# Seven products of halves in place of eight for the second feed-forward product, and the residual stream parked in DRAM

## Chip, cores, metric

One core of one Trainium2 chip. The metric is the device time of the whole kernel in microseconds, median of the runs shown; lower is better. Engines are named as in the profile: PE is TensorE (PEld its weight loads), DVE is VectorE, ACT is ScalarE, POOL is GpSimd, SP is SyncE, which here only issues DMAs.

## What is computed

Two layers of a transformer trunk over 512 latent tokens and 256 context tokens of 1024 channels. Each layer has four mixers on one input projection, an output projection with a residual layer norm, and then a feed-forward block with a second residual layer norm. The change touches only the feed-forward block:

```python
def channel_mlp(h, w1, w2):
    return jnp.square(jax.nn.relu(h @ w1)) @ w2
...
x = layer_norm_affine(DN_ALPHA * x + m[2] * y, ln1_g[l], ln1_b[l])
f = channel_mlp(modulate(x, m[3], m[4]), w_ff1[l], w_ff2[l])
x = layer_norm_affine(DN_ALPHA * x + m[5] * f, ln2_g[l], ln2_b[l])
```

`w_ff1` is 1024 x 4096, `w_ff2` is 4096 x 1024, all float32. In layer 0 the context tokens go through the same block, so N = 768 rows; in layer 1 only the latent tokens do, N = 512.

## The kernel before

**Arithmetic.** A float32 product is made of three products in the type fp32r: each operand is split into a high part (an ACT copy into fp32r) and a low part (a DVE subtraction, operand minus high part), and `mm3` (L135) issues high x high, high x low, low x high into the same PSUM bank. A "split" below is this pair of one ACT and one DVE instruction; for a weight piece it is `load_w` (L154), ACT at L162, DVE at L165, on 128 x 1024 elements.

**Order.** The program is written as straight code; a planner takes the instructions in about program order, whichever is ready first by its own timing model, and fixes each engine's queue. On the chip every queue runs in that fixed order, with waits on semaphores.

**Feed-forward block, `ffn` (L181).** The 4096 hidden columns go in eight chunks `c` of 512. `ff1(c)` (L208) makes four hidden tiles of 128 columns x N tokens: 24 matmuls of 512 columns each, in layer 0 another 24 of 256 columns, into a two-bank PSUM tile from `P2`; ACT evicts it with a relu into `r` (`T` tile); `square` (L201) makes the high part on ACT and, with two DVE instructions, the low part, in two `Z` tiles. `ff2(c, fs)` (L1277) multiplies by 512 rows of `w_ff2`: for each half `n` of the 1024 output columns and each token tile (6 in layer 0, 4 in layer 1) `ff2_tile` (L1262) issues 4 x 3 matmuls of 512 columns into one bank from `PA`, then DVE multiplies the bank by the gate row (L1274) and adds it to the residual tile `x` or `xc` in SBUF (L1275). The loop at L1299 issues `ff1(c + 1)` ahead of `ff2(c)`. In chunk 7 `ff2` goes tile by tile, POOL does the additions, and `done(j)` (L1448) starts the closing layer norm of the tile.

**Pools of tiles.** `pw` (`N_W` = 8) holds four weight pieces as high and low parts, `pr` (`N_RAW` = 4) four raw pieces as loaded, `pz` (`N_Z` = 18) the 128 x 768 `Z` tiles, `pt` (`N_T` = 6) the `T` tiles, `px` 6 tiles for `x` and `xc`, `pg` 4 `G` tiles of 128 x 1024 for gate and norm rows. PSUM has 3 banks in `PA`, 1 in `PF`, 2 x 2 in `P2`. A tile that reuses a slot waits until the last reader of the former one is through. Weights come by DMA on SP's queue (`load`, L114), gate and norm rows on ACT's queue (`bcast_rows`, L1304), where `rows2` (L1437) fetches all four.

## Time and profile before

| | us |
|---|---|
| median of 3 runs | 1571.38 (1569.65 to 1572.05) |
| profiled execution, its time | 1570.16 |
| its span | 1568.4 |
| PE busy | 1481.3 (94% of the span) |
| DVE busy | 922.7 (59%) |
| ACT busy | 565.7 (36%) |
| POOL busy | 222.0 (14%) |

Busy time is the union of an engine's instructions over the span. The feed-forward matmuls run from about 382 to 924 us (layer 0) and from about 1202 to 1553 us (layer 1); the mixers, with POOL's softmax scaling among them, lie outside these stretches.

### The profile page before, as it was taken

The page shows a single profiled execution, that of the slowest core. Times are in us where ns is not written, and L with a number is a line of the kernel's source. Part 1 is how long each engine was busy: PE and PEld are TensorE (multiplying, and loading weights), DVE is VectorE, ACT ScalarE, POOL GpSimd, SP SyncE. Part 2 cuts the span into 40 slices and gives each one's busy share as a digit, 9 for nine tenths or more (in the row PEclk, how much of TensorE's full clock was granted, in tenths as well). Part 3 has the DMA queues.
Part 4 walks back from the last instruction along what each step waited for, and adds up shares of the span by engine and source line. Part 5 has one row for each costly group of instructions (what it writes and reads, how often), then busy time and mean ns, then how long its engine had stood idle before and what let it go on. Part 6 is the DMA issues. An engine that isn't in the chain of part 4 may idle for free.

```text
span 1568.4 us, 23456 instructions
## 1 busy us (share of the span) xinstructions
PE 1481.3 (94%) x9438; PEld 1246.7 (79%) x9438; DVE 922.7 (59%) x1615; ACT 565.7 (36%) x1000; POOL 222.0 (14%) x244
## 2 busy tenths in 40 slices
PE   5899889999999999999999989989998999999996
PEld 3689677787988888888888868867776888888885
DVE  4385755547545445454454798675645656655557
ACT  4433555524621221312113156355625433222322
POOL 1021334223000000000000062143222000000003
PEclk9999999999999999999999999999998999999998
DMA  8441366362232121211211223235363433333221
GB/s 296 152 120 55 112 219 195 108 242 89 81 108 65 49 76 54 76 59 55 81 55 67 81 94 111 64 109 178 120 208 108 147 95 95 95 101 92 88 81 54
DMA packets 148069, 169.93 MB, mean 108 GB/s; under 512 B 8776, under 2 KB 96248, under 8 KB 147960
## 3 DMA queue, kind: packets, MB, share of 16 engines
q1 hardware_dynamic: 137912, 149.94, 30.7%
q10 hardware_dynamic: 10048, 18.49, 3.5%
q8 instruction: 74, 1.21, 0.3%
q14 instruction: 35, 0.29, 0.1%
HBM read 164.19 MB, written 4.22 MB: 107 GB/s over the span
## 4 chain that ended last, share of the span: by engine, by line
PE 84%; DVE 7%; DMA 3%; ACT 2%; issue 1%; POOL 1%; SPq 0%; ACTq 0%; POOLq 0%; DVEq 0%
PE ff L133 54%; PE wo L133 5%; PE wb L133 3%; PE o L133 3%; PE pT L188 2%; PE wa L133 2%; PE ada L133 2%; PE wp L133 2%; PE wu L133 2%; PE wq L133 2%; PE sm L133 2%; DMA wada<-in_w_ada 1%; DVE nmax L533 1%; PE wk L133 1%; PE hT L188 1%
## 5 line engine op out<-in xcount | busy, mean ns | idle before, releaser
L162 ACT ACTIVATE hiw<-raww 128x1024 fp32r<-128x1024 f32 x120 | 126.8, 1062 | 565.8 <-PE ff L133 565.8
L165 DVE TENSOR_TENSOR low<-raww,hiw 128x1024 fp32r<-128x1024 f32 x120 | 146.3, 1223 | 245.3 <-ACT hiw L162 245.3
L133 PE MATMUL ff<-low,fh 128*128 128x512 f32 x640 | 249.0, 389 | 0.0
L133 PE MATMUL ff<-hiw,fl 128*128 128x512 f32 x640 | 249.0, 389 | 0.0
L133 PE MATMUL ff<-hiw,fh 128*128 128x512 f32 x640 | 247.9, 389 | 0.0
L133 PE MATMUL ff<-hl,hiw 128*128 128x512 f32 (+1 forms) x672 | 237.9, 354 | 0.0
L133 PE MATMUL ff<-hh,hiw 128*128 128x512 f32 (+1 forms) x672 | 237.8, 354 | 0.0
L133 PE MATMUL ff<-hh,low 128*128 128x512 f32 (+1 forms) x672 | 237.7, 354 | 0.0
L1274 DVE TENSOR_TENSOR fft<-ff,gate 128x512 f32<-128x512 f32 x160 | 110.0, 687 | 100.2 <-PE ff L133 100.2
L133 PEld LDWEIGHTS ff<-hh,hiw 128*128 128x128 f32 x672 | 127.1, 189 | 17.9
L133 PEld LDWEIGHTS ff<-hl,hiw 128*128 128x128 f32 x672 | 127.1, 189 | 17.7
L133 PEld LDWEIGHTS ff<-hh,low 128*128 128x128 f32 x672 | 127.0, 189 | 17.7
L133 PEld LDWEIGHTS ff<-hiw,fl 128*128 128x128 f32 x640 | 120.1, 188 | 25.0
L133 PEld LDWEIGHTS ff<-hiw,fh 128*128 128x128 f32 x640 | 120.2, 188 | 24.8
L133 PEld LDWEIGHTS ff<-low,fh 128*128 128x128 f32 x640 | 120.1, 188 | 24.7
L1275 POOL TENSOR_TENSOR x<-x,fft 128x512 f32<-128x512 f32 x14 | 20.3, 1452 | 837.5 <-DVE fft L1274 832.5
L547 POOL TENSOR_SCALAR p<-p,rec 128x768 f32<-128x768 f32 (+3 forms) x80 | 63.1, 793 | 142.0 <-DVE rec L546 132.1
L1275 DVE TENSOR_TENSOR x<-x,fft 128x512 f32<-128x512 f32 x114 | 78.7, 690 | 2.9
L133 PE MATMUL ada<-wada,sc 128*32 128x128 f32 x1536 | 60.7, 295 | 20.0 <-DMA wada<-in_w_ada 20.0
L133 PEld LDWEIGHTS ada<-wada,sc 128*32 128x32 f32 x1536 | 41.8, 116 | 34.1 <-DMA wada<-in_w_ada 13.1
L188 PE MATMUL pT<-ident,p 128*128 128x128 f32 x368 | 55.9, 279 | 9.9 <-ACT pT L555 4.4
L133 PE MATMUL wo<-lowo,yh 128*128 128x512 f32 x160 | 62.5, 390 | 0.5 <-DVE lowo L165 0.5
(335 smaller groups left out, 2749.7 us busy)
## 6 DMA issues: line engine op xcount, KB each, us to landing
raww<-in_w_ff SPq DMA_DIRECT2D x120, 512.0 KB, 4.2
wada<-in_w_ada SPq DMA_DIRECT2D x96, 512.0 KB, 4.6
rawwo<-in_w_out SPq DMA_DIRECT2D x16, 512.0 KB, 6.1
rawz<-in_w_ff SPq DMA_DIRECT2D x8, 512.0 KB, 5.6
rawwb<-in_w_in SPq DMA_DIRECT2D x12, 256.0 KB, 4.1
gate<-grow ACTq DMA_DIRECT2D x6, 512.0 KB, 6.8
badab<-in_b_ada SPq DMA_DIRECT2D x36, 64.0 KB, 3.9
x<-in_x SPq DMA_DIRECT2D x4, 512.0 KB, 4.4
```

Source lines behind the costliest of these rows:

```text
L133: return self.pinned(self.nc.tensor.matmul(out, lhsT, rhs, start=start, stop=stop))
L162: i = nc.scalar.activation(out=hi, in_=raw, func=AF.Copy)
L165: nc.vector.tensor_tensor(out=lo, in0=raw, in1=hi.bitcast(F32), op=ALU.subtract)
L188: return self.pinned(self.nc.tensor.transpose(out, in_, self.ident if ident is None else ident))
L533: nc.vector.tensor_reduce(out=nm, in_=S[:, lo:hi], axis=AX.X, op=ALU.max, negate=True)
L547: nc.gpsimd.tensor_scalar(out=p[:, :keep], in0=p[:, :keep], scalar1=rec, scalar2=1.0, op0=ALU.mult, op1=ALU.mult)
L1274: nc.vector.tensor_tensor(out=t, in0=ps, in1=g[:, sl], op=ALU.mult)
L1275: eng.tensor_tensor(out=xt[:, sl], in0=xt[:, sl], in1=t, op=ALU.add)
```

## The change

For chunks 0 to 6 the product of the chunk's hidden activations (N x 512) with its 512 x 1024 weights is made by Strassen's scheme in Winograd's form. The activations are cut into halves of tokens (`half` = 384 in layer 0, 256 in layer 1; `HT` = 3 or 2 token tiles) and of hidden columns (even and odd tiles), the weights into the same halves of rows and halves of output columns. Seven products of halves, each `HT` x 2 x 3 matmuls of 512 columns, take the place of eight.

The parts: `operands` squares `r` on POOL, forms sums and differences of halves on POOL in `T` tiles, and splits seven pairs of halves on ACT and DVE, two pairs ahead of the loop body and one after each product (`more`). `weights` loads four raw quarters, forms four differences on POOL, in place, and splits seven pieces (before: four). `ff2_chunk` adds each product's banks, straight from PSUM, to one or two accumulators in SBUF: ten additions for each token tile of a half. Four quarters of the result lie in `acc` (the six `X` slots), a part common to three of them in `base` (two or one `G` tiles). In chunk 0 the first write of each is an ACT copy. Since `acc` takes the slots of the residual stream, `x` is written to DRAM (`xr`) and fetched again after the product of chunk 6; there DVE adds `base`, POOL multiplies by the gate row, DVE adds the residual. Chunk 7 stays as it was, and its `square` too, but `ff1(7)` is now issued after the product of chunk 6. The rows of the closing norm are fetched late (`rows2(1)`), since `base` takes their slots.

```diff
...
+        N = NL + NC if full else NL
+        half = N // 2
+        HT = half // 128
+
...
+                rs.append(r)
+            return rs
 
         def ff1_first():
 
...
+        def operands(rs):
+
+            pool = nc.gpsimd
+            for r in rs:
+                pool.tensor_tensor(out=r[:, :N], in0=r[:, :N], in1=r[:, :N], op=ALU.mult)
+            q = []
+            for p in range(2):
+                tmp = self.T("fsum", 768)
+                e, o = rs[2 * p], rs[2 * p + 1]
+                q.append((e[:, :half], o[:, :half], e[:, half:N], o[:, half:N], tmp[:, :half], tmp[:, half:N]))
+
+            def halves(k):
+                res = []
+                for v in q:
+                    z = self.Z("fop")
+                    hi, lo = z[:, :half], z[:, half:N]
+                    nc.scalar.activation(out=hi, in_=v[k], func=AF.Copy)
+                    nc.vector.tensor_tensor(out=lo, in0=v[k], in1=hi.bitcast(F32), op=ALU.subtract)
+                    res.append((hi, lo))
+                return res
+
+            def sums(o, a, b, op):
+                for v in q:
+                    pool.tensor_tensor(out=v[o], in0=v[a], in1=v[b], op=op)
+
+            yield halves(0)
+            sums(4, 2, 3, ALU.add)
+            yield halves(4)
+            sums(5, 4, 0, ALU.subtract)
+            yield halves(5)
+            sums(4, 1, 5, ALU.subtract)
+            yield halves(4)
+            sums(2, 0, 2, ALU.subtract)
+            yield halves(2)
+            yield halves(1)
+            yield halves(3)
+
+        def weights(c):
+
+            pool = nc.gpsimd
+
+            def raw(odd, n):
+                t = self.pr.tile([128, 2, 512], F32, name=self.nm("raww2"), tag="raw")
+                self.load(out=t, in_=w2[:, 4 * c + odd:4 * c + 4:2, 512 * n:512 * n + 512])
+                return t
+
...
+            def diff(o, a, b):
+                pool.tensor_tensor(out=o, in0=a, in1=b, op=ALU.subtract)
+
+            b11, b12, b22, b21 = raw(0, 0), raw(0, 1), raw(1, 1), raw(1, 0)
+            yield halves(b11)
+            diff(b11, b12, b11)
+            yield halves(b11)
+            diff(b11, b22, b11)
+            yield halves(b11)
+            diff(b12, b22, b12)
+            yield halves(b22)
+            yield halves(b12)
+            yield halves(b21)
+            diff(b21, b21, b11)
+            yield halves(b21)
+
+        def ff2_chunk(c, left, acc, base, more):
+
+            B = weights(c)
+            seen = set()
+
+            def add(ps, key, sl):
+                if c == 0 and key not in seen:
+                    seen.add(key)
+                    nc.scalar.activation(out=sl, in_=ps, func=AF.Copy)
+                else:
+                    nc.vector.tensor_tensor(out=sl, in0=ps, in1=sl, op=ALU.add)
+
+            for i, to in enumerate((("11", "B"), ("12", "22"), ("B",), ("12",), ("21", "22"), ("11",), ("21",))):
+                if i % 2 == 0:
+                    banks = [self.PA("ff2") for _ in range(HT)]
+                else:
+                    big = self.P2("ff2")
+                    banks = [big[:, 0:512], big[:, 512:1024]]
+                    if HT > 2:
+                        banks.append(self.PF("ff2") if i == 3 else self.P2("ff2")[:, 0:512])
+                W, a = next(B), left[i]
+                for t in range(HT):
+                    for p in range(2):
+                        self.mm3(
+                            banks[t], [h[:, 128 * t:128 * t + 128] for h in a[p]],
+                            [h[:, p, :] for h in W], p == 0, p == 1,
+                        )
+                    for q in to:
+                        if q == "B":
+                            sl = base[t]
+                        else:
+                            n = int(q[1]) - 1
+                            sl = acc[HT * (int(q[0]) - 1) + t][:, 512 * n:512 * n + 512]
+                        add(banks[t], (q, t), sl)
+                more()
 
...
-        def ff2(c, fs):
-            if c < NCH - 1:
-                for n in range(2):
-                    Ws = ff2_w(c, n)
-                    for tl in tiles:
-                        ff2_tile(fs, Ws, n, tl, nc.vector)
-            else:
-                Ws = [ff2_w(c, n) for n in range(2)]
-                self.ends = []
-                if l == 0:
-                    self.wb_first = self.wb_z(1)
-                for j, tl in enumerate(tiles):
-                    for n in range(2):
-                        eng = nc.vector if l == DEPTH - 1 and j == len(tiles) - 1 else nc.gpsimd
-                        ff2_tile(fs, Ws[n], n, tl, eng, self.last_mm if j + n else None)
-                    done(j)
-
-        cur = ff1_first()
-        gl, gc = rows2()
-        tiles = [(128 * i, x[i], gl) for i in range(LT)]
-        if full:
-            tiles += [(NL + 128 * i, xc[i], gc) for i in range(CT)]
-        for c in range(NCH):
-            nxt = ff1(c + 1) if c + 1 < NCH else None
-            ff2(c, cur)
-            cur = nxt
+        rs = ff1_first()
+        big = [self.G([128, 1024], "base") for _ in range((HT + 1) // 2)]
+        base = [big[t // 2][:, 512 * (t % 2):512 * (t % 2) + 512] for t in range(HT)]
+        gl, gc = rows2(0)
+
+        xr = self.pd.tile([N, D], F32, name=self.nm("xr"), tag=self.nm("xr"))
+        for j, t in enumerate(x + (xc or [])):
+            nc.sync.dma_start(out=xr[128 * j:128 * j + 128, :], in_=t)
+        acc = [self.X([128, 1024], "acc") for _ in range(N // 128)]
+        left = list(operands(rs))
+        for c in range(NCH - 1):
+            nxt, ops = [], None
+            if c < NCH - 2:
+                ops = operands(ff1(c + 1))
+                nxt += [next(ops), next(ops)]
+
+            def more():
+                if ops is not None:
+                    nxt.extend([z for z in [next(ops, None)] if z is not None])
+
+            ff2_chunk(c, left, acc, base, more)
+            left = nxt
+
+        rs = ff1(NCH - 1)
+        for j, t in enumerate(acc):
+            raw = self.pr.tile([128, 1024], F32, name=self.nm("rawx"), tag="raw")
+            self.load(out=raw, in_=xr[128 * j:128 * j + 128, :])
+            for n in range(2):
+                if j >= HT or n:
+                    sl = t[:, 512 * n:512 * n + 512]
+                    nc.vector.tensor_tensor(out=sl, in0=sl, in1=base[j % HT], op=ALU.add)
+            nc.gpsimd.tensor_tensor(out=t, in0=t, in1=gl if j < LT else gc, op=ALU.mult)
+            nc.vector.tensor_tensor(out=t, in0=t, in1=raw, op=ALU.add)
+        rows2(1)
+        fs = [square(r, N) for r in rs]
+        tiles = [(128 * j, t, gl if j < LT else gc) for j, t in enumerate(acc)]
+        Ws = [ff2_w(NCH - 1, n) for n in range(2)]
+        self.ends = []
+        if l == 0:
+            self.wb_first = self.wb_z(1)
+        for j, tl in enumerate(tiles):
+            for n in range(2):
+                eng = nc.vector if l == DEPTH - 1 and j == len(tiles) - 1 else nc.gpsimd
+                ff2_tile(fs, Ws[n], n, tl, eng, self.last_mm if j + n else None)
+            done(j, tl[1])
 
     def bcast_rows(self, src, name):
 
...
+            def rows2(late):
+                if not late:
+                    return self.bcast_rows(gr2[0], "gate"), None if last else self.bcast_rows(gr2[1], "gate")
                 norm2.append(self.bcast_rows(A["ln2_g"][l], "ln2g"))
                 norm2.append(self.bcast_rows(A["ln2_b"][l], "ln2b"))
-                return norm2[0], norm2[1]
 
...
```

## Rows read from the trace of the kernel before

**Rows 1.** The page: engines' busy shares of the span, chain that ended last

```profile
PE 1481.3 (94%) x9438; PEld 1246.7 (79%) x9438; DVE 922.7 (59%) x1615; ACT 565.7 (36%) x1000; POOL 222.0 (14%) x244
...
PE ff L133 54%; PE wo L133 5%; PE wb L133 3%; PE o L133 3%; PE pT L188 2%; PE wa L133 2%; PE ada L133 2%; PE wp L133 2%; PE wu L133 2%; PE wq L133 2%; PE sm L133 2%; DMA wada<-in_w_ada 1%; DVE nmax L533 1%; PE wk L133 1%; PE hT L188 1%
```

**Rows 2.** Chain of waits (start us, length us, engine, tile): both feed-forward stretches

```profile
421.84 489.47 PE ff L133 x2506
...
1217.08 322.97 PE ff L133 x1463
```

**Rows 3.** Busy time by stretch: a first product, a second, chunks, a gap

```profile
core 0: us, PE busy (x) PEld busy (x) DVE busy (x) ACT busy (x) POOL busy (x), PEclk, DMA share, GB/s
400.00:466.00 66.00, 64.41 (x433) 58.67 (x432) 34.49 (x50) 31.31 (x55) 0.55 (x1) 1.00 0.28 89
430.10:463.43 33.33, 33.33 (x195) 29.50 (x194) 15.33 (x16) 9.95 (x13) 0.00 (x0) 1.00 0.35 111
463.43:496.06 32.63, 32.63 (x146) 27.03 (x145) 20.09 (x27) 5.63 (x6) 0.00 (x0) 1.00 0.16 49
598.00:664.00 66.00, 66.00 (x338) 56.56 (x337) 33.08 (x40) 14.68 (x17) 0.00 (x0) 1.00 0.22 64
1190.00:1234.00 44.00, 39.91 (x303) 35.91 (x304) 25.87 (x55) 28.11 (x56) 2.92 (x5) 0.89 0.47 146
...
1366.00:1410.00 44.00, 44.00 (x196) 36.42 (x195) 25.65 (x33) 12.96 (x16) 0.00 (x0) 1.00 0.32 96
```

**Rows 4.** Groups by line: DVE by size; busy us, mean ns, idle before

```profile
L165 DVE TENSOR_TENSOR low<-raww,hiw 128x1024 fp32r<-128x1024 f32 x120 | 146.3, 1223 | 245.3 <-ACT hiw L162 245.3
L1274 DVE TENSOR_TENSOR fft<-ff,gate 128x512 f32<-128x512 f32 x160 | 110.0, 687 | 100.2 <-PE ff L133 100.2
...
L1083 DVE TENSOR_TENSOR w1z<-rawz,w1z 128x384 fp32r<-128x384 f32 x16 | 8.2, 552 | 7.7 <-ACT w1z L1082 7.7
...
L388 DVE TENSOR_TENSOR hl<-hfull,hh 128x256 fp32r<-128x256 f32 x72 | 29.8, 422 | 26.7 <-ACT hfull L387 26.1
```

**Rows 5.** Instructions in time (start us, length us): DVE back to back

```profile
1304.68 1.21 DVE L165 TENSOR_TENSOR low<-raww,hiw 128x1024 fp32r<-128x1024 f32 x1
1305.82 0.68 DVE L1275 TENSOR_TENSOR x<-x,fft 128x512 f32<-128x512 f32 x1
...
1295.63 0.68 DVE L1274 TENSOR_TENSOR fft<-ff,gate 128x512 f32<-128x512 f32 x1
1296.23 0.68 DVE L1205 TENSOR_TENSOR fl<-relu,fh 128x512 fp32r<-128x512 f32 x1
```

**Rows 6.** Instructions in time: POOL, four operations in a row (x4)

```profile
334.08 5.04 POOL L1179 TENSOR_TENSOR x<-x,wot 128x512 f32<-128x512 f32 x4 [22.80 <-DVE wot L1178]
```

**Rows 7.** Instructions in time: DVE and POOL at once, in three places

```profile
336.01 0.67 DVE L1178 TENSOR_TENSOR wot<-wo,gate 128x512 f32<-128x512 f32 x1
...
929.11 1.27 DVE L342 SCALAR_TENSOR_TENSOR xc<-xc,bmv,ln2g 128x1024 f32<-128x1024 f32 x1
...
929.34 2.17 POOL L1275 TENSOR_TENSOR xc<-xc,fft 128x512 f32<-128x512 f32 x1 [2.57 <-DVE fft L1274]
...
930.43 2.15 DVE L165 TENSOR_TENSOR lowb<-rawwb,hiwb 128x1024 fp32r<-128x1024 f32 x1
...
1549.59 1.29 POOL L1275 TENSOR_TENSOR x<-x,fft 128x512 f32<-128x512 f32 x1
...
1549.77 1.13 DVE L313 SCALAR_TENSOR_TENSOR nmr<-bmv,brs 128x1 f32<-128x1 f32 x1
```

**Rows 8.** Instructions in time: ACT at the end of a first product

```profile
463.51 1.06 ACT L162 ACTIVATE hiw<-raww 128x1024 fp32r<-128x1024 f32 x1 [5.70 <-PE ff L133]
464.47 0.79 ACT L1199 ACTIVATE relu<-ff 128x768 f32<-128x768 f32 x1
465.30 0.85 ACT L1203 ACTIVATE fh<-relu 128x768 fp32r<-128x768 f32 x1
```

**Rows 9.** The page, DMA issues (count, KB each, us to landing): weights

```profile
raww<-in_w_ff SPq DMA_DIRECT2D x120, 512.0 KB, 4.2
```

More of the change, by code (lines that the diff above doesn't have):

```diff
@@ L1215, in ff1 @@
                     ff1_mm(ps[:, NL:NL + NC], hC, 0, W)
-                n = NL + NC if full else NL
                 r = self.T("relu", 768)
-                relu(r, 0, ps[:, :n])
-                fs.append(square(r, n))
-            return fs
+                relu(r, 0, ps[:, :N])
+                rs.append(r)
+            return rs
         def ff1_first():
@@ L1250, in ff1_first @@
                             relu(rs[f - 1 + i], NL, big[:, 512 * i:512 * i + 256])
-            return [square(r, NL + NC if full else NL) for r in rs]
+            return rs
+        def operands(rs):
[30 more added lines that the diff above has]
+            yield halves(3)
@@ new lines, in weights, with halves @@
+        def weights(c):
[4 more added lines that the diff above has]
+                return t
+            def halves(t):
+                hi = self.pw.tile([128, 2, 512], F32R, name=self.nm("hiw2"), tag="W")
+                lo = self.pw.tile([128, 2, 512], F32R, name=self.nm("low2"), tag="W")
+                nc.scalar.activation(out=hi, in_=t, func=AF.Copy)
+                nc.vector.tensor_tensor(out=lo, in0=t, in1=hi.bitcast(F32), op=ALU.subtract)
+                return hi, lo
+            def diff(o, a, b):
[12 more added lines that the diff above has]
+            yield halves(b21)
@@ L1435, in run, with done @@
             norm2 = []
-            def rows2():
-                norm2.append(self.bcast_rows(gr2[0], "gate"))
-                norm2.append(None if last else self.bcast_rows(gr2[1], "gate"))
+            def rows2(late):
+                if not late:
+                    return self.bcast_rows(gr2[0], "gate"), None if last else self.bcast_rows(gr2[1], "gate")
                 norm2.append(self.bcast_rows(A["ln2_g"][l], "ln2g"))
                 norm2.append(self.bcast_rows(A["ln2_b"][l], "ln2b"))
-                return norm2[0], norm2[1]
             hLn, hCn = (None, None) if last else (hl(), hc())
             xn = []
-            def done(j):
-                t = x[j] if j < LT else xc[j - LT]
-                g2, b2 = norm2[2:]
+            def done(j, t):
+                g2, b2 = norm2
                 if last:
```

2 lines of the change are left out of this document (1 added, 1 removed).

## Prediction

> **What bounds the kernel now.** I read the page's shares first: PE is busy for 94% of the span and 54% of the chain that ended last is feed-forward matmul [rows 1]. Then the chain in order of time: in layer 0 it stays on feed-forward matmuls for 489.5 us without a break, in layer 1 for 323.0 us [rows 2]. So within these stretches a matmul taken away is time saved, as long as nothing else becomes late. Who is next is read from the stretches [rows 3]: in a layer 0 chunk of 66 us DVE is busy for 33.1, ACT 14.7, POOL 0; in layer 1 in 44 us DVE 25.7, ACT 13.0, POOL 0. DVE is the one to watch; POOL is free. The second product alone (32.63 us in layer 0) has 20.1 us of DVE, the first (33.33 us) 15.3.
>
> **What goes.** 144 matmuls of 512 columns fill 32.63 us [rows 3]: 0.2266 us each. Layer 0 loses 18 of 144 per chunk (32.63 becomes 28.55, -4.08), layer 1 12 of 96 (21.75 becomes 19.03, -2.72). Seven chunks of both: 47.6 us, the ceiling.
>
> **Prices of what comes.** Back to back, a DVE split of 1024 columns takes 1.14 us from start to start, a 512-column operation 0.60 [rows 5]; lengths are 1.22 and 0.69, for 384 and 256 columns 0.55 and 0.42 [rows 4]; with the same overlap of 0.08 I take steps of 1.15, 0.61, 0.47 and 0.34. An ACT split takes 1.06 [rows 8]. POOL's two-input operation takes 1.26 us per 512 columns, four in a row 5.04 [rows 6]; it is not shown for other widths, so I scale: 1024 2.5 us, 768 1.9, 384 0.95, 256 0.63. A bound from the other side is that half of it is a fixed cost (0.63 + 0.63 per 512: 1.9 us for 1024, but 0.95 for 256); the totals below would hardly move. The Trainium skill (GPSIMD Engine Reference, 3.1) gives 4497 ns for 2048 columns, so an estimate of 2.25 us for 1024; no row shows that width. By it the one difference per stretch is 0.3 us shorter and the sum below ends some 3 us lower.
>
> Per chunk, layer 0 / layer 1: DVE gets 30 / 20 additions (18.3 / 12.2 us), 11 splits of weights (12.7) and 14 low halves (6.6 / 4.8): 37.6 / 29.7 us, for a PE chunk of 61.9 / 40.8. POOL gets four squares, eight sums, four differences: 7.6 + 7.6 + 10 = 25 / 20 us. Neither exceeds PE. But two things make the mean misleading.
>
> **First: the load is uneven.** The additions fall into the second product alone, and a weight piece can only be split when a slot comes free: ACT's split in the trace starts 0.1 us after the matmuls that held the slot, having waited 5.70 us for them [rows 8]. With four slots and a piece every 4.1 or 2.7 us instead of every 8, five splits fall into each second product: products 3 to 6 and the first piece of the next first product. So do the low halves of six of the seven operand pairs. Until PE can go on with the next first product DVE must do: in layer 1, 18 additions (11.0), 5 splits (5.75), 12 low halves (4.1): 20.8, and 1.3 at the start in which it waits for ACT's first split: 22.1 us, where PE wants 19.0. Layer 0: 27 (16.5), 5.75, 12 (5.6), 1.3: 29.2 us, where PE wants 28.55. On top comes a chain at the end: the sixth piece must be split before POOL may overwrite it (2.5 us), then ACT (1.06) and DVE (1.15) make the seventh: 4.7 us against products of 4.1 and 2.7, with the sixth split itself late behind additions. I give it 1.2 us, between 0 (split early) and 4.7. So 30.4 and 23.3 us without any collision, against 32.63 and 21.75 before.
>
> **Second: POOL and DVE collide.** Where both work from SBUF, one waits for the other's whole instruction [rows 7]: at 929.11 DVE runs 1.27 us on two SBUF operands and POOL's 1.26 us operation, begun at 929.34, lasts 2.17; the DVE split at 930.43, behind it, lasts 2.15 instead of 1.22; at 1549.77 a one-column DVE operation takes 1.13 us until POOL ends. An operation that reads PSUM and one SBUF operand is untouched: at 336.01, amid four POOL operations, 0.67 us [rows 6, 7]. So the new additions don't collide, the splits and low halves do. Before, POOL was empty in these stretches [rows 3]. In the second product POOL has one square, eight sums and one difference: 8.8 us in layer 1 (40% of about 22), 12 us in layer 0 (39% of about 31). The 17 splits and low halves meet a running POOL operation that often; its mean remainder (sum of squares over twice the sum) is 0.63 and 0.71 us; met at random that is 4.3 and 4.7 us. I take half, since POOL mostly gets in when DVE turns to additions, which then cover it: 2.1 and 2.4. Bounds: 0, and all of POOL's 8.8 and 12. Who waits for it: everything behind a blocked split in DVE's fixed order, the additions that free PSUM banks and the pieces PE needs next. So a full chunk's second product comes to 25.4 us in layer 1 (+3.7) and 32.8 in layer 0 (+0.2).
>
> **Sum.** Chunks 1 to 5: 5 x 0.2 + 5 x 3.7 = +19.5. In chunk 0 ACT takes half of the additions (9.2 / 6.1 us off DVE): PE sets the pace, -3.5 and -2.0. Chunk 6 has no operands to prepare, but follows chunk 5's second product with no first product between to build its weights: -3.0 and 0. Steady part: +11.
>
> Once per layer: chunk 0's seven operand pairs are a chain of POOL, ACT and DVE of about 16 us (layer 0: squares to 4.6, then about 2 to 3.3 per pair) beside two hidden tiles' matmuls (16.7 us); 1 us each layer, bounds 0 and 8. At the end `ff1(7)` now runs straight into the product of chunk 7. Relu 0.79, ACT square 0.85 [rows 8], DVE about 0.95 (from 384 and 256 columns [rows 4]) were covered by a product before; now the first nine matmuls cover 2.0. `ff1(7)` also has to hold the refetch and `base` work: in layer 1 DVE 8.3 for it, 4.9 for squares, 9.2 for splits, 22.4 us in 21.8, with 10 us of POOL beside; in layer 0 28 in 33. I take 3 and 5 us; bounds 0 and 10 each. Together +10.
>
> At no cost: residual tiles of 512 KB out and in on SP's queue (DMA share 0.22 to 0.32 [rows 3], landing 4.2 us [rows 9]), with weights queued behind them but three pieces in hand; it would cost about 4 us a layer if they weren't. ACT (19 to 21 us a chunk) stays under half. The late `rows2(1)` can hold ACT's queue until `base` is read, behind it the squares of chunk 7; that is in the 3 and 5 us.
>
> 1570.2 + 11 + 10 = 1591 us by the profiled execution; the median is 1.2 above it: **1592 us**.
>
> **Rivals.** *Collisions and order hidden (chance 0.32).* For: PE's DVE work has a whole first product to catch up in, a late split matters only after about three products, and the planner may put urgent splits ahead. Then each second product costs PE's time and 1 us: 7 x (-3.1 - 1.7) = -34, with 8 once: 1545 us. Against: its model must know POOL's waits, which traces show and program order ignores. The Trainium skill (Perfetto Trace Analysis, Identifying Performance Opportunities) holds that improving the most-contended engine improves the kernel; taken alone that is the whole 47.6, 1524 us, and the rows bear it out only while PE stays the one that others wait for.
>
> *Lockstep (0.12), slower.* If collisions are met in full at random and not half hidden, because the fixed orders keep meeting, it is +2.5 and +5.9 per full chunk, 5 x 8.4 = 42, less 8.5 for chunks 0 and 6, and 15 once: 1570 + 49 + 1 = 1620 us. It decides from about 3 us of waits a stretch on; every POOL us in the way would give 1670.
>
> *The clock falls (0.05).* Between 1190 and 1234 PE idles 4.1 of 44 us and the granted clock is 0.89, partly at 1.2 GHz for 2.4: 4.8 us of full speed lost. Between 400 and 466 it idles 1.6 us and keeps 1.00 [rows 3]. If PE's stalls in each full layer 1 chunk come to look like the former, that adds 5 x 4.8 = 24: 1616 us.
>
> *A wash (0.08).* Layer 0's gain pays for layer 1's loss: with collisions at a fifth of random, 1571 us.
>
> **How the numbers follow.** The forecast (1577 to 1608) has 0.43. Range 1540 to 1630: down to the middle of the first rival, up past the lockstep's value; what is left out is the planner at its best and POOL wholly in the way. A measurement of this kernel can tell 0.2% (3 us) from no change. Faster 0.32, same 0.08, slower 0.60.
>
> **What would show it.** PE with 126 or 84 matmuls per second product, its idle time put down to DVE splits of weights or to ACT behind them, chiefly in products 4 to 6; layer 1's chunks longer than 43.5 us (2 x 21.75) and layer 0's near 66; splits with a median well over 1.22 us, additions from PSUM at 0.69; POOL busy about 20 to 25 us a chunk. Wrong if layer 1's chunks come out near 41 us with splits at 1.22, or if the idle time lies on DMA or on POOL's weight differences.

## The result and the profile after

The changed kernel takes 1638.1 us (median of 4 runs, 1634.1 to 1640.5) against 1570.7 for the kernel before on the same chip: a ratio of 1.0426, 95% interval 1.0401 to 1.0451. Slower was forecast, but at 1592 us with 1630 as the upper end, so 46 us are to be explained. Most of them lie in places where the sum had come out at nothing or nearly nothing.

The page of the changed kernel, busy times and four of its groups (busy us, mean ns | idle before, releaser):

```profile
PE 1484.5 (91%) x9228; PEld 1226.5 (75%) x9228; DVE 1102.6 (67%) x1811; ACT 661.7 (40%) x1207; POOL 600.9 (37%) x478
...
L133 PE MATMUL ff<-hiw,fop 128*128 128x512 f32 x980 | 325.0, 406 | 36.3 <-DVE acc L1338 35.6
...
L1308 DVE TENSOR_TENSOR low<-raww,hiw 128x1024 fp32r<-128x1024 f32 x98 | 136.7, 1397 | 159.7 <-ACT hiw L1307 159.4
...
L1338 DVE TENSOR_TENSOR acc<-ff,acc 128x512 f32<-128x512 f32 x260 | 167.9, 676 | 12.3 <-PE ff L133 12.2
...
L1312 POOL TENSOR_TENSOR raww<-raww,raww 128x1024 f32<-128x1024 f32 x56 | 137.3, 2452 | 86.7 <-DVE low L1308 67.5
```

PE has 210 matmuls fewer than before [rows 1] and yet 3 us more of busy time, because some of them ran at the lower clock; its share falls from 94% to 91%. What PE waits for is plain: of the 36.3 us of waiting before this group, two thirds of the Strassen matmuls, 35.6 end with a DVE addition out of PSUM (L1338), the instruction that gives a bank back. (The other third, `ff<-low,fop`, waits 6.7 us, for weight splits.) The weight splits went from 1223 to 1397 ns on average [rows 4], the additions from PSUM stayed at 676.

Busy time by stretch, for two second products of layer 0 (534 and 603), the two last Strassen products together (809), `ff1(7)` (879), the last product (921), and two full chunks of layer 1 (1333, 1380):

```profile
core 0: us, PE busy (x) PEld busy (x) DVE busy (x) ACT busy (x) POOL busy (x), PEclk, DMA share, GB/s
...
534.20:569.40 35.20, 29.89 (x128) 23.30 (x126) 34.03 (x49) 14.46 (x21) 10.39 (x7) 1.00 0.33 90
...
602.90:638.10 35.20, 31.50 (x128) 24.43 (x126) 34.05 (x49) 13.95 (x21) 10.39 (x7) 0.95 0.33 90
808.90:879.30 70.40, 60.76 (x255) 47.89 (x253) 69.23 (x92) 21.84 (x28) 23.08 (x13) 0.96 0.26 76
879.30:921.30 42.00, 37.99 (x193) 32.80 (x194) 29.73 (x20) 7.73 (x9) 15.46 (x5) 0.87 0.40 130
921.30:959.00 37.70, 35.03 (x147) 27.87 (x145) 29.64 (x49) 9.75 (x18) 18.82 (x15) 0.95 0.28 91
1333.40:1380.40 47.00, 42.93 (x181) 34.55 (x180) 35.90 (x45) 19.06 (x29) 23.49 (x16) 0.96 0.30 90
1380.40:1429.10 48.70, 44.37 (x181) 35.20 (x181) 36.10 (x45) 19.08 (x29) 23.50 (x16) 0.93 0.29 87
```

The two second products of layer 0 are the key there. In both DVE is busy for 34.0 of 35.2 us: it is full. PE's clock is 1.00 in the one and 0.95 in the other (a part of it at 1.2 GHz for 2.4, after PE's waits), and they are equally long: the lower clock only used up time in which PE would have waited. Before, the same stretch took 32.63 us with DVE busy for 20.1 [rows 3].

Layer 1 is different. DVE works without a break through most of the second product (1334.5 to 1360.1), which makes PE wait, but then waits itself, 2.46 us, for PE; over the chunk it is busy for 36 of 47 us. So a slower PE is paid for there. The full chunks alternate between 47.0 us at a mean clock of 0.96 and 48.7 at 0.93, with the same work and the same waits. What the clock takes of them by these rows is 1.9 and 3.4 us of full speed; the difference, 1.5 us, is nearly that of the two lengths, 1.7. Before, the clock was 1.00 in such a chunk [rows 3].

By the first matmul of each stage (leaving out a few that the queue pulls ahead) the 70.0 us between the two profiled spans (1638.4 and 1568.4) divide as follows; the middle column is what the prediction's terms give for the stage:

| stage | predicted | measured |
|---|---|---|
| ahead of `ff1(1)`, layer 0 (at 436.8, before at 430.1) | 0 | +6.7 |
| layer 0, chunk 0 | -2.5 | -2.1 |
| layer 0, chunks 1 to 4 (68.7 us each, before 66.0) | +0.8 | +10.7 |
| layer 0, from `ff1(6)` to the last matmul (183.5 us, before 164.8) | +0.2 | +18.7 |
| from there to `ff1(1)` of layer 1 (307.2, before 302.1) | 0 | +5.1 |
| layer 1, chunk 0 | -1.0 | +1.5 |
| layer 1, chunks 1 to 4 (47.8 us each, before 43.5) | +14.8 | +17.3 |
| layer 1, from chunk 5 on | +8.7 | +11.9 |

(0.2 us lie behind the last matmul.)

### The profile page after: what moved, and what is told of

It reads as the page before. It is cut to its first block, busy times and chain, and to the rows that moved or that the text cites. A ratio compares the mean times of both kernels' runs of the same rounds, so it can differ in the third digit from the quotient of the medians.

```text
span 1638.4 us, 23881 instructions
## 1 busy us (share of the span) xinstructions
PE 1484.5 (91%) x9228; PEld 1226.5 (75%) x9228; DVE 1102.6 (67%) x1811; ACT 661.7 (40%) x1207; POOL 600.9 (37%) x478
## 5 line engine op out<-in xcount | busy, mean ns | idle before, releaser
L133 PE MATMUL ff<-hiw,fop 128*128 128x512 f32 x980 | 325.0, 406 | 36.3 <-DVE acc L1338 35.6
L133 PEld LDWEIGHTS ff<-hiw,fop 128*128 128x128 f32 x980 | 191.3, 195 | 87.9 <-DVE acc L1338 25.3
L1308 DVE TENSOR_TENSOR low<-raww,hiw 128x1024 fp32r<-128x1024 f32 x98 | 136.7, 1397 | 159.7 <-ACT hiw L1307 159.4
L1262 POOL TENSOR_TENSOR relu<-relu 128x768 f32<-128x768 f32 (+1 forms) x56 | 91.2, 1631 | 318.3 <-ACT relu L1199 318.3
L133 PE MATMUL ff<-low,fop 128*128 128x512 f32 x490 | 199.2, 406 | 6.7 <-DVE low L1308 6.7
L1338 DVE TENSOR_TENSOR acc<-ff,acc 128x512 f32<-128x512 f32 x260 | 167.9, 676 | 12.3 <-PE ff L133 12.2
L1312 POOL TENSOR_TENSOR raww<-raww,raww 128x1024 f32<-128x1024 f32 x56 | 137.3, 2452 | 86.7 <-DVE low L1308 67.5
L133 PEld LDWEIGHTS ff<-low,fop 128*128 128x128 f32 x490 | 95.5, 195 | 32.1 <-DVE low L1308 13.0
L1275 DVE TENSOR_TENSOR fop<-relu,fop 128x384 fp32r<-128x384 f32 (+1 forms) x112 | 87.0, 801 | 39.9 <-ACT fop L1274 39.9
L165 DVE TENSOR_TENSOR low<-raww,hiw 128x1024 fp32r<-128x1024 f32 x64 | 82.0, 1289 | 14.6 <-ACT hiw L162 14.5
L1275 DVE TENSOR_TENSOR fop<-fsum,fop 128x384 fp32r<-128x384 f32 (+1 forms) x84 | 75.0, 914 | 7.3 <-ACT fop L1274 7.3
```

What stands on the lines that cost most here:

```text
L133: return self.pinned(self.nc.tensor.matmul(out, lhsT, rhs, start=start, stop=stop))
L165: nc.vector.tensor_tensor(out=lo, in0=raw, in1=hi.bitcast(F32), op=ALU.subtract)
L1262: pool.tensor_tensor(out=r[:, :N], in0=r[:, :N], in1=r[:, :N], op=ALU.mult)
L1275: nc.vector.tensor_tensor(out=lo, in0=v[k], in1=hi.bitcast(F32), op=ALU.subtract)
L1308: nc.vector.tensor_tensor(out=lo, in0=t, in1=hi.bitcast(F32), op=ALU.subtract)
L1312: pool.tensor_tensor(out=o, in0=a, in1=b, op=ALU.subtract)
```

## The experiments

Times are given as ratios to the kernel before, run on the same chip beside each, with 95% intervals; 0.001 is 1.6 us. The changed kernel itself stands at 1.0426.

**What paces the second product: two runs that leave work out.**

Without GpSimd:

```diff
-                pool.tensor_tensor(out=r[:, :N], in0=r[:, :N], in1=r[:, :N], op=ALU.mult)
...
-            sums(4, 2, 3, ALU.add)
...
+            for k in (0, 2, 3, 1, 2, 1, 3):
+                yield halves(k)
...
-            diff(b11, b12, b11)
```

> Left out: everything that GpSimd does in the feed-forward of the changed kernel (squares, sums of halves, differences of weight blocks); ScalarE and VectorE split the unsummed halves instead, so their counts and TensorE's are those of the changed kernel. Theory (VectorE's own work paces the second product: in 671.5 to 706.8 us it was busy 34.1 of 35.3 us, of which about 31.8 would be left without meetings with GpSimd): a full chunk of layer 0 falls from 68.7 to about 65.5 us, of layer 1 from 47.8 to about 44.5, and the whole from 1638 to about 1595 us. Rival (GpSimd, by its meetings with VectorE and by the chains that wait for its sums, is the main cost): chunks of 62 and 41 us, close to TensorE's own 61.9 and 40.8, and a whole of about 1550 us. Rival (TensorE's clock): no change of the chunks.

One addition a product:

```diff
-            for i, to in enumerate((("11", "B"), ("12", "22"), ("B",), ("12",), ("21", "22"), ("11",), ("21",))):
+            for i, to in enumerate((("11",), ("22",), ("B",), ("12",), ("21",), ("11",), ("21",))):
```

> Left out: three of the ten additions out of PSUM for each pair of tiles (each product is added to one target alone), 9 a chunk in layer 0 and 6 in layer 1; splits, sums, GpSimd's work and TensorE's are those of the changed kernel. Theory (VectorE's own work paces the second product): 9 x 0.60 us = 5.4 us less in a chunk of layer 0, so 68.7 to about 63.3 us, and 6 x 0.60 = 3.6 less in layer 1, 47.8 to about 44.2, the whole about 1584 us. Rival (GpSimd and the chains behind its sums): at most 1 us a chunk, the whole about 1630 us.

Measured: 1.0060 (1.0044 to 1.0076), 1582.5 us, without GpSimd, and 1.0051 (1.0035 to 1.0066), 1580.7 us, with one addition a product. Full chunks of layers 0 and 1: 65.0 and 43.0 us without GpSimd, 62.9 and 43.7 with fewer additions. The stretch of one second product of layer 0 and of one chunk of layer 1 in the run without GpSimd, and of one second product of layer 0 in the run with fewer additions:

```profile
533.50:565.10 31.60, 28.77 (x129) 23.53 (x127) 30.30 (x47) 13.37 (x19) 0.00 (x0) 1.00 0.27 84
...
1315.80:1358.80 43.00, 41.66 (x180) 33.53 (x180) 29.48 (x46) 18.00 (x29) 0.00 (x0) 1.00 0.32 98
```

```profile
532.20:561.70 29.50, 28.79 (x128) 23.53 (x127) 28.10 (x38) 14.18 (x21) 10.87 (x7) 1.00 0.33 94
```

In layer 0 the theory holds. Nine additions fewer shorten the product by 5.8 us (35.25 to 29.5; 5.4 expected), until PE's own 28.6 us are nearly reached. Taking all of GpSimd away shortens it by 3.7, and DVE is still busy for 30.3 of 31.6 us. The share of the meetings is read from DVE's groups in such a stretch, of the changed kernel (534.2 to 569.4) and of the run without GpSimd (533.5 to 565.1):

```profile
L1308 DVE TENSOR_TENSOR low<-raww,hiw 128x1024 fp32r<-128x1024 f32 x4 | 5.7, 1413 | 4.3 <-ACT hiw L1307 4.3
L1275 DVE TENSOR_TENSOR fop<-fsum,fop 128x384 fp32r<-128x384 f32 x6 | 5.2, 899 | 0.0
...
L1275 DVE TENSOR_TENSOR fop<-relu,fop 128x384 fp32r<-128x384 f32 x6 | 3.2, 544 | 0.0
```

```profile
L1271 DVE TENSOR_TENSOR fop<-relu,fop 128x384 fp32r<-128x384 f32 x10 | 5.3, 548 | 0.1
L1291 DVE TENSOR_TENSOR low<-raww,hiw 128x1024 fp32r<-128x1024 f32 x4 | 4.9, 1217 | 5.6 <-ACT hiw L1290 5.6
```

Four splits at 1413 ns for 1217, and six low halves of sums at 899 for 544: 0.8 and 2.1, together 2.9 us. (The other 0.8 us: in the run without GpSimd two of the 12 low halves fall outside the stretch.) How such a meeting looks in the changed kernel, POOL first, then DVE:

```profile
677.91 1.02 POOL L1281 TENSOR_TENSOR fsum<-fsum,relu 128x384 f32<-128x384 f32 x1
678.88 2.01 POOL L1281 TENSOR_TENSOR relu<-relu 128x384 f32<-128x384 f32 x1
```

```profile
678.01 2.00 DVE L1308 TENSOR_TENSOR low<-raww,hiw 128x1024 fp32r<-128x1024 f32 x1
679.93 2.47 DVE L1338 TENSOR_TENSOR acc<-ff,acc 128x512 f32<-128x512 f32 x4
```

The split at 678.01 waits for POOL's sum and takes 2.00 us for 1.22; POOL's next sum then waits for the split and takes 2.01 for 1.02; the four additions from PSUM behind it, 2.47 us together, are not touched. The Trainium skill (SBUF — State Buffer, "SBUF: two separate sides") has this as an exclusive lock that whoever starts first holds for the whole instruction; the rows agree.

In layer 1 the theory was too low on GpSimd: without it a chunk falls by 4.8 us, more than by the additions (4.1), to 43.0, where the rival had 41. DVE's busy time in a chunk goes from 35.9 us (the stretch at 1333 above) to 29.5. Of these 6.4 us only 2.2 lie in the second product (1333.4 to 1362.5, where four splits and 12 low halves take longer than 1.21 and 0.41 us); and the clock, 0.96 and 0.93 in the changed kernel, is 1.00 here. The 2.2 us and the 2.6 that the clock takes on average together come to the 4.8; no run takes the two apart. A meeting in layer 1, with POOL, DVE and PE in the same moment:

```profile
1441.81 2.36 POOL L1312 TENSOR_TENSOR raww<-raww,raww 128x1024 f32<-128x1024 f32 x1 [3.36 <-DVE low L1308]
```

```profile
1442.86 1.60 DVE L1275 TENSOR_TENSOR fop<-fsum,fop 128x256 fp32r<-128x256 f32 x1
...
1444.71 1.28 DVE L1338 TENSOR_TENSOR acc<-ff,acc 128x512 f32<-128x512 f32 x2
```

```profile
1446.13 0.47 PE L133 MATMUL ff<-hiw,fop 128*128 128x512 f32 x1 [3.67 <-DVE acc L1338]
```

A low half of 0.41 us takes 1.60 beside POOL's weight difference, the additions stand behind it, and PE waits 3.67 us for the bank, 1.2 of them by this meeting. That wait is there once in every full chunk of layer 1.

**The same saving with nothing left out: accumulate in PSUM.** The third, fourth and seventh products need only be summed with the first, second and fifth:

```diff
-            for i, to in enumerate((("11", "B"), ("12", "22"), ("B",), ("12",), ("21", "22"), ("11",), ("21",))):
...
+            for i, (to, onto) in enumerate((("11", None), ("22", None), ("B", 0), ("12", 1), ("22", None),
+                                            ("11", None), ("21", 4))):
+                if onto is not None:
+                    banks = held[onto]
...
+                                self.pinned(nc.tensor.matmul(banks[t], l[u], r[v], start=False,
...
```

> Nothing is left out; the third, fourth and seventh products are accumulated in the PSUM banks that the first, second and fifth have left, so that each product needs one addition in place of ten for seven. Theory (VectorE's additions pace the second product): the chunks are those of the run with one addition a product that left the others out, 62.9 us in layer 0 and 43.7 in layer 1, the whole about 1583 us. Rival (a product that goes onto banks still to be read by an addition makes TensorE wait for it): 1 to 3 us more a chunk, 64 to 66 in layer 0, the whole about 1600.

Measured: 1.0104 (1.0088 to 1.0121), 1590.7 us, between theory and rival. Layer 0's chunks come to 63.0 us, the theory's number, 3 us under the kernel before. Layer 1's come to 46.0 on average, not 43.7: there the rival is right, PE waits 2.0 us at a product that goes onto a bank whose addition is still queued, and 0.8 for a split. (The Trainium skill, PSUM — Partial Sum Buffer, "PSUM: the matmul accumulator", says that a partial sum may be read, synchronised, in the middle of an accumulation group; this is what the run does.)

**DVE's order at the end of a chunk.** In the changed kernel, DVE around the end of the product that begins at 534, and PE's first matmul of the next first product:

```profile
561.89 1.21 DVE L165 TENSOR_TENSOR low<-raww,hiw 128x1024 fp32r<-128x1024 f32 x1
...
564.09 1.21 DVE L165 TENSOR_TENSOR low<-raww,hiw 128x1024 fp32r<-128x1024 f32 x1
...
565.69 1.87 DVE L1338 TENSOR_TENSOR acc<-ff,acc 128x512 f32<-128x512 f32 x3
567.49 1.21 DVE L165 TENSOR_TENSOR low<-raww,hiw 128x1024 fp32r<-128x1024 f32 x1
568.62 1.27 DVE L1338 TENSOR_TENSOR acc<-ff,acc 128x512 f32<-128x512 f32 x2
```

```profile
569.44 0.47 PE L133 MATMUL ff<-hh,hiw 128*128 128x512 f32 x1 [2.08 <-DVE acc L1338]
```

Three splits for the *next* first product (L165), of which PE needs only one at once, stand ahead of the addition that begins at 568.62, whose bank PE needs now.

```diff
...
-                            self.gate if f < 8 else None)
+                            self.gate if f < 8 else None, self.last_add if full and f >= 8 and f % 4 else None)
...
-                    nc.vector.tensor_tensor(out=sl, in0=ps, in1=sl, op=ALU.add)
+                    d = nc.vector.tensor_tensor(out=sl, in0=ps, in1=sl, op=ALU.add); i == 6 and full and self.after(d, self.last_add); self.last_add = d if i < 6 else self.last_add
```

> Nothing is left out; only the order on VectorE in layer 0 is changed: the additions of the sixth product come ahead of those of the seventh, and the splits of pieces 2 to 4 of the next first product behind both. Theory (VectorE's order at the end of a chunk holds TensorE: at 569.44 us the first matmul of the next first product waited 2.08 us for an addition of the sixth product, which stood behind two weight splits and the additions of the seventh): 2.1 us less in a full chunk of layer 0, 68.7 to about 66.6, the whole down by about 10 us to 1628. Rival (VectorE has no slack and the same work is late elsewhere): chunks within 0.5 us of 68.7, the whole at 1638.

Measured: 1.0272 (1.0252 to 1.0291), 1616.0 us, 24 us less: twice what was expected, and elsewhere. A product of full chunks in this run, one at full clock and one not, and then the end of layer 0 (the last two Strassen products, `ff1(7)`, the last product):

```profile
530.00:564.70 34.70, 31.43 (x129) 24.71 (x128) 29.95 (x43) 13.41 (x21) 10.39 (x7) 0.95 0.26 76
```

```profile
666.00:699.00 33.00, 29.73 (x128) 23.48 (x127) 29.95 (x43) 13.40 (x20) 10.38 (x7) 1.00 0.27 80
800.20:865.20 65.00, 60.73 (x255) 48.23 (x254) 63.80 (x85) 20.96 (x28) 22.90 (x13) 0.97 0.24 73
865.20:898.50 33.30, 33.30 (x194) 29.50 (x192) 32.45 (x26) 8.82 (x10) 15.49 (x5) 1.00 0.51 164
898.50:936.20 37.70, 34.92 (x147) 28.00 (x146) 31.35 (x54) 12.37 (x21) 17.99 (x15) 0.95 0.36 120
```

At full clock the product takes 33.0 us, 2.2 less, as the theory says. Three of the four full chunks had the lower clock instead and came to 34.6: PE's waits earlier in the product (3.3 us, unchanged) are followed by 0.95, and most of what the order wins the clock takes. The larger gain is at the end: 65.0 + 33.3 + 37.7 = 136.0 us for 150.1. (Another 6 us lie ahead of layer 0 and between the layers, which this order doesn't touch; why, no run settles.) There, in the changed kernel, PE's first matmul of `ff1(7)`, at 879.27, waits 5.65 us for the second of these, an addition of the sixth product:

```profile
877.85 0.68 DVE L1418 TENSOR_TENSOR acc<-acc,base 128x512 f32<-128x512 f32 x1
878.45 0.68 DVE L1338 TENSOR_TENSOR acc<-ff,acc 128x512 f32<-128x512 f32 x1
```

From 863.3 us on six additions of `base` (L1418) and four weight splits stand ahead of it. In the run with the new order that wait is gone, and as the residual's tiles are through earlier the last weights are issued at 881.9 us and not at 896.5.

**One layer alone.** Layer 1 keeps the second product of the kernel before:

```diff
...
+        if not full:
+            cur = [square(r, N) for r in rs]
...
+                            ff2_tile(cur, Ws, n, tl, nc.vector)
```

> One part alone: the change as it stands in layer 0, and layer 1 with the second product of the kernel before; nothing is left out. Theory (each layer's loss is its own: in layer 1 the chunks are 17.2 us and the end 11.6 us longer than before, and 4.6 us lie between the layers): 1638 less 29 to 33, 1605 to 1610 us, so about half of the loss lies in each layer. Rival (the losses of layer 1 follow from layer 0, by the clock or by work pushed ahead): 1620 or more.

Measured: 1.0219 (1.0206 to 1.0232), 1608.5 us. Each layer's loss is its own, about half each.

**The residual stream.** Three runs: its writes behind the conditioning loads in SP's queue; its way back into `Z` tiles; and without it.

```diff
...
-            nc.sync.dma_start(out=xr[128 * j:128 * j + 128, :], in_=t)
+            self.after(nc.sync.dma_start(out=xr[128 * j:128 * j + 128, :], in_=t), self.last_load)
```

> One thing changed: SyncE's queue writes the residual to DRAM only after the loads of the conditioning weights; no other engine's order changes. Theory (these writes wait for the norm and hold back the conditioning loads, 2.3 us on TensorE's path ahead of the feed-forward of layer 0 and about 4 in layer 1): the whole falls by about 6 us, to 1632. Rival (the loads come late for another reason, their buffers or the transfers themselves): within 2 us of 1638.

Measured: 1.0392 (1.0373 to 1.0410), 5 us less within intervals of 3 on either side. SP's issues ahead of the feed-forward of layer 0, first of the changed kernel, then of this run, each with the PE matmul that waits for the load:

```profile
382.09 0.32 SPq L1395 DMA_DIRECT2D xr<-x  x1
382.46 2.26 SPq L116 DMA_DIRECT2D badab<-in_b_ada  x4
384.81 3.14 SPq L116 DMA_DIRECT2D wada<-in_w_ada  x4
```

```profile
389.81 1.08 PE L133 MATMUL ada<-wada,sc 128*32 128x128 f32 x16 [2.87 <-DMA wada<-in_w_ada]
```

```profile
386.39 2.67 SPq L116 DMA_DIRECT2D wada<-in_w_ada  x4
389.16 3.14 SPq L1395 DMA_DIRECT2D xr<-x  x4
```

```profile
390.50 0.64 PE L133 MATMUL ada<-wada,sc 128*32 128x128 f32 x16 [0.94 <-DMA wada<-in_w_ada]
```

From the last mixers' work (the conditioning matmuls at 383.1 and 385.7) to `ff1(1)` it is 53.7 us in the changed kernel, 50.6 here and 51.4 before: the theory holds for layer 0, 3 us. For layer 1 it falls: that stretch is 42.6, 42.7 and 42.9 us in the three. The 5.1 us between the layers arise earlier: 2.8 in the first projections of layer 1, 1.5 in its mixers, 1.1 in its output projection; why, no run settles.

```diff
-            raw = self.pr.tile([128, 1024], F32, name=self.nm("rawx"), tag="raw")
...
+                raw = self.Z("rawx", F32)[:, :512]
+                self.load(out=raw, in_=xr[128 * j:128 * j + 128, 512 * n:512 * n + 512])
...
```

> One thing changed: at the end of a layer the residual comes back from DRAM in half rows into the tiles that held operands of the second product, not into the four buffers that weights are loaded into. Theory (the end of layer 0, chunks 5 to 7, took 18.9 us more than before, of layer 1 11.6 more, in part because the weights of the last chunk wait for these buffers, 25.7 us at one place, and ScalarE's relu is queued behind that wait): 4 to 8 us less in layer 0, 2 to 5 less in layer 1, the whole about 1629 us. Rival (the additions and multiplications that bring the residual in cost the end, wherever it is loaded to): within 2 us of 1638.

Measured: 1.0384 (1.0368 to 1.0401), 7 us less. In the changed kernel SP's queue, ACT and PE at the end of layer 0:

```profile
869.87 23.61 SPq L116 DMA_DIRECT2D rawx<-xr  x6
```

```profile
900.26 1.06 ACT L162 ACTIVATE hiw<-raww 128x1024 fp32r<-128x1024 f32 x1 [25.72 <-DMA raww<-in_w_ff]
901.22 0.79 ACT L1199 ACTIVATE relu<-ff 128x768 f32<-128x768 f32 x1
```

```profile
902.07 0.80 PE L133 MATMUL ff<-hh,hiw 128*128 128x512 f32 x1 [4.00 <-ACT relu L1199]
```

Six residual tiles pass through the four weight buffers, so the next weights are only issued at 896.5; ACT, whose order was fixed, waits 25.7 us for them with a relu behind, and PE 4.0 us for the relu's bank. With the `Z` tiles both waits go: `ff1(7)` and the last product take 35.8 + 36.1 us for 42.0 + 37.7, 7.7 less. In layer 1 nothing is gained (theory: 2 to 5), and the two last Strassen products still take 70.3.

And the residual left out:

```diff
-            nc.sync.dma_start(out=xr[128 * j:128 * j + 128, :], in_=t)
...
-            self.load(out=raw, in_=xr[128 * j:128 * j + 128, :])
...
-            nc.vector.tensor_tensor(out=t, in0=t, in1=raw, op=ALU.add)
```

> Left out: the residual's way out to DRAM, its way back and its addition in both layers; the multiplication by the gate and the additions of the shared part stay. Theory (the residual's traffic costs by where it stands in queues: about 3 us ahead of the feed-forward of layer 0, 8 to 12 at its end, 2 to 4 in layer 1): about 1622 us. Rival (it costs nothing, and VectorE's order alone makes the ends long): within 5 us of 1638.

Measured: 1.0335 (1.0321 to 1.0348), 14 us less: about 7 at the end of layer 0, 4 in layer 1, the rest ahead of the two layers; 1622 was expected. The wait at the start of `ff1(7)` stays, at 5.05 us: it is not the residual that makes it.

**All of it together, and where it pays.** The PSUM accumulation, the residual's two ways, and the squares on ACT:

```diff
-                pool.tensor_tensor(out=r[:, :N], in0=r[:, :N], in1=r[:, :N], op=ALU.mult)
+                nc.scalar.activation(out=r[:, :N], in_=r[:, :N], func=AF.Square)
```

> Nothing is left out; the PSUM accumulation of the run beside it, the residual's way back through the operand tiles, its way out behind the conditioning loads, and the squares on ScalarE in place of GpSimd. Theory (VectorE's additions, its meetings with GpSimd, and the ends): 6 us less by the way back, 3 by the way out, up to 1 us a chunk by fewer meetings: about 1570 us, no faster than the kernel before, since what is saved in the chunks is spent at the ends. Rival (ScalarE, which gets 3.4 us more in a chunk, becomes late with relu and the upper halves): no better than the PSUM accumulation alone, about 1583.

> Nothing is left out; as the run with all four edits, but layer 1 keeps the second product of the kernel before. Theory (layer 0 has 4.08 us a chunk to win and layer 1 2.72, of which its longer end, 11.6 us, takes more than half): layer 0's chunks at 62.5 us against 66.0 before, its end about 5 us longer than before, layer 1 as before: about 1560 us, faster than the kernel before by some 10. Rival (the end of layer 0 and the hand-over to layer 1 cost as much as the chunks save): about 1571.

Measured: 1.0040 (1.0025 to 1.0055), 1579.9 us, with all edits in both layers; 0.9965 (0.9952 to 0.9978), 1568.1 us, with all edits in layer 0 alone. Layer 0's chunks are 62.5 us in both. Layer 1's, at 44.4, are still longer than the 43.5 before; there the scheme doesn't pay. Both runs are slower than the theories had it (1570 and 1560) and near the rivals (1583 and 1571). What is left is again the end of layer 0:

```profile
778.40:845.30 66.90, 57.52 (x255) 47.10 (x253) 65.21 (x76) 22.37 (x29) 29.72 (x14) 0.95 0.39 118
```

```profile
845.29 0.77 PE L133 MATMUL ff<-hh,hiw 128*128 128x512 f32 x1 [9.38 <-DVE acc L1338]
```

Two orders were tried against that wait. All additions in the order of the products, splits and residual behind:

```diff
...
+                    d = nc.vector.tensor_tensor(out=sl, in0=ps, in1=sl, op=ALU.add); seen and c and self.after(d, self.last_add); self.last_add = d; seen.add(key)
```

> Nothing is left out; the run with all four edits in layer 0 alone, with VectorE's additions of layer 0 in the order of the products, and the splits of pieces 2 to 4 of the next first product and the residual's additions behind them. Theory (what is left of layer 0's end is VectorE's order: at 845.3 us of that run TensorE waited 9.37 us for an addition that stood behind seven operations of the residual): that wait goes, and with it some us of a lower clock behind it; the pair of last products 66.9 to about 57.5 us, the last chunk 2 to 4 us less, the whole about 1557 us, 1.0% under the kernel before. Rival (the residual's operations, now behind the additions, are late for the last chunk instead): within 3 us of 1568.

Measured: 1.0066 (1.0053 to 1.0078), 1584.7 us, 16 us worse than without, and worse than theory and rival had it. In the second product of a full chunk DVE, held to that order, now idles 2.5 us in four waits for ACT (0.7, 0.4, 0.9 and 0.4 us). Without that order none of these is there; in place of the first two DVE did additions of a later product (`base`). Full chunks go from 62.5 to 64.6 us, and in `ff1(7)` PE waits for a split that was put behind:

```profile
877.03 0.80 PE L133 MATMUL ff<-hh,low 128*128 128x512 f32 x1 [7.03 <-DVE low L165]
```

So only one thing was ordered, the last sixth product ahead of the last seventh and of the residual:

```diff
...
+                    d = nc.vector.tensor_tensor(out=sl, in0=ps, in1=sl, op=ALU.add); self.adds[i, key[1]] = d; [self.after(d, self.adds[5, t]) for t in range(HT) if c == NCH - 2 and i == 6]
...
+                    d = nc.vector.tensor_tensor(out=sl, in0=sl, in1=base[j % HT], op=ALU.add); [self.after(d, self.adds[5, t]) for t in range(HT)]
```

> Nothing is left out; the run with all four edits in layer 0 alone, and one order on VectorE added, at the end of layer 0 only: the additions of the last sixth product come ahead of those of the last seventh and of everything that brings the residual in. No other order is fixed, so the chunks stay at 62.5 us. Theory (the wait of 9.37 us at 845.3 us of that run is an addition of the sixth product that stood behind the residual's operations): the pair of last products falls from 66.9 to about 58 us, the last chunk by 0 to 2, the whole to about 1558 us, 1.0% under the kernel before. Rival (what is put behind, the splits of the last first product among it, is late instead, as in the run where all additions were in order and the last first product waited 7.0 us for a split): about 1566, as without the order.

Measured: 0.9942 (0.9929 to 0.9956), 1565.4 us. The end of layer 0 in this run, and one of its waits:

```profile
776.50:833.80 57.30, 57.30 (x254) 47.22 (x254) 50.26 (x63) 20.98 (x28) 19.06 (x10) 1.00 0.43 138
833.80:867.10 33.30, 33.30 (x193) 29.49 (x192) 33.30 (x31) 9.10 (x11) 16.77 (x6) 1.00 0.20 63
867.10:911.10 44.00, 37.30 (x146) 28.96 (x145) 35.86 (x56) 9.81 (x18) 18.76 (x15) 0.88 0.29 96
```

```profile
877.55 0.79 PE L133 MATMUL ff<-hiw,fl 128*128 128x512 f32 x1 [2.43 <-DVE fl L1205]
```

Theory and rival are both right in part: the two Strassen products run at PE's own pace (57.3 us for 66.9, no wait), `ff1(7)` at its 33.3, but the squares of chunk 7 are now behind the residual on DVE, and the last product takes 44.0 us for 38.0. Half of the gain is given back; the version is 0.6% faster than the kernel before.

## Why the sign was right and the size wrong

**What goes, and the prices.** PE's 0.2266 us a matmul held (57.3 us for the 252 matmuls of two products where nothing waits). So did the DVE prices. POOL's difference of 1024 columns took 2.45 us on average; I had scaled 2.5 from my rows, and the estimate of 2.25 from the Trainium skill (GPSIMD Engine Reference, 3.1) was lower than what the trace shows.

**Second product of layer 0, 32.8 us predicted, 35.25 measured.** The failed step is the count of what DVE has to do "until PE can go on with the next first product". I let three additions and two splits fall behind that point: 27 and 5, 27.9 us of DVE work. In the fixed order 29 additions and 7 splits lay ahead of it: 34.0 us busy, less 2.9 of meetings, so 31.1. That is 3.2 us more. Meetings were 2.9 for 2.4 (half of random: the choice was nearly right), DVE's own idle time 1.2 where I had 1.3 and 1.2: 1.3 less. 3.2 + 0.5 - 1.3 = 2.4 us, the whole difference. The run that put the sixth product's additions first restores the order I had assumed, and at full clock its product takes 33.0 us (in part by luck: DVE waits 1.5 us for PE at its end, so the sums agree better than their parts). The mechanism was right, then; I had taken my own order for the planner's.

**Ends of the layers.** The failed step here is "I take 3 and 5 us", with bounds of 10: layer 0's end cost 18.7 us. Two causes were shown: `base`'s additions and weight splits placed on DVE ahead of additions that PE's banks wait for (14 us came back with the order); and the weight buffers taken by the residual, with a relu queued on ACT behind the late weights (7.7 us with other buffers; the two overlap). Beside these waits the clock was 0.87 to 0.96; what it costs there by itself no run separates. I had counted the work against the length of `ff1(7)` and found room; what decides is that a late operation in a full, fixed queue stands ahead of an urgent one. I gave chunk 6 a gain of 3.0 us for having no operands to prepare; `base`'s and the residual's work took that place.

**"At no cost".** The residual's way out and back, with its addition, cost 14 us in all, 2 to 3 of them ahead of layer 0 by its place in SP's queue. My bound of "about 4 us a layer" looked at the weights behind it in the feed-forward; the conditioning loads ahead of it, and the buffers on the way back, I did not look at. Of the 6.7 us ahead of `ff1(1)`, 4.4 had arisen by 311 us, where the change touches nothing; in the other runs `ff1(1)` began anywhere between 430.3 and 438.1, with the same source for that part, and what sets it stays open. So does the cause of the 5.1 us between the layers: together 9 to 10 of the 46 us.

**Layer 1** came out near the forecast in its full chunks (+4.3 for +3.7), though by errors that cancel. The meetings were 2.2 us for 2.1, so half of random was right. But the lower clock, which the sum left out (a rival at 0.05), takes 1.9 and 3.4 us of a chunk by turns: about 10 us in chunks 1 to 4. In their place I had 1.2 us for a chain, and DVE's work too high: without GpSimd, and at full clock, a chunk takes 43.0 us, where my terms without meetings and chain give 43.9 (22.1 + 21.75).

**The rivals.** The lockstep's 1620 was nearest, but not by its mechanism: meetings were met at little over half of random in layer 0, at half in layer 1. The clock did fall, mean 0.960 for 0.984; in layer 0's full products it cost nothing as long as DVE set the pace, in layer 1's it cost about half of what that rival had. "A wash" was added up wrongly: a fifth of random in the sum's own terms gives about 1578 us, not 1571. "Collisions and order hidden" failed because the planner did not put the urgent operation first. The rule of the Trainium skill (Perfetto Trace Analysis, Identifying Performance Opportunities) that goes by the most-contended engine, taken over the whole span, would have given 1524; once PE had less to do, DVE was full in the second product of layer 0, though over the span it was busy for 67% against PE's 91%.

**What I had said would show it:** PE's waits were there, from the sixth product of a full chunk on and at the first matmul behind the last, where I had named the fourth to sixth; but on additions that free PSUM banks, hardly on weight splits or ACT. The splits' median stayed at 1.23 us; only their mean rose, to 1.40, as 27 of 98 were long.

## What to carry to other kernels

Saving matmuls by adding vector work paid here only where the vector engine had room in that very stretch: count what it must finish before the next matmul that needs a bank, in the order its queue is fixed in, not in the order you would choose. What helped most was to make fewer of those operations (accumulate in PSUM, three additions in ten fewer), and next to order only the one addition that someone waits for; ordering all of them made it slower. Price what is moved "aside" by the queue it stands in and the buffer it passes through: here that was a fifth of the loss.

## What the hardware did that I had not expected

Two second products of the same work took the same 35.2 us at a granted clock of 1.00 and of 0.95 (PE busy 29.9 and 31.5): where DVE sets the pace, the slower clock is free, and it becomes dear as soon as DVE is relieved (33.0 us at 1.00 and 34.7 at 0.95 in the run with the new order). In layer 1, where DVE waits for PE at the end of the product, the same chunk took 47.0 us at 0.96 and 48.7 at 0.93. And a meeting of DVE and POOL costs both: 2.00 us for a split of 1.22 and, right behind it, 2.01 for a sum of 1.02.
